# Seven products of a block pair summed in PSUM chains, pairs interleaved, and rotated q fetched in fewer transfers

## The chip, the cores and the metric

The kernel runs on one core of a Trainium2 chip. The metric is device time in microseconds for one execution; lower is better. Before the change it is 1741.86 us (median of three runs, 1740.02 to 1743.96). The core has five engines with a queue each: TensorE (PE, matrix products), VectorE (DVE), ScalarE (ACT), GpSimd (POOL) and SyncE (SP), which here issues nearly all transfers. Products land in PSUM, eight banks of 128 x 512 fp32; VectorE and ScalarE read them there.

## The reference

One gated block on x of 1024 positions by 1024 channels: a normalised x times a wide weight `w_in`, whose columns feed two branches, an mLSTM (a) and a differential attention (b), which are mixed, projected and normalised.

```python
h = rmsnorm(x, norm_g[layer])
proj = jnp.einsum('bsd,de->bse', h, w_in[layer])
(a_q, a_k, a_v, a_o, a_z, a_g, b_q, b_k, b_v, b_z, g_a, g_b) = jnp.split(proj, _split_points(), axis=-1)
qk = jax.nn.silu(centred_depthwise_conv(jnp.concatenate([a_q, a_k], axis=-1), ml_conv_w[layer]))
...
y_a = hm * jax.nn.sigmoid(a_o) * jax.nn.silu(a_z)
...
dq = apply_rope(b_q.reshape(B, S, DA_HEADS, 2, DA_QK_DIM), positions)
dk = apply_rope(b_k.reshape(B, S, DA_HEADS, 2, DA_QK_DIM), positions)
att = diff_attention(dq, dk, da_v, lam)
...
mix = (jax.nn.sigmoid(g_a + gb[0]) * jnp.einsum('bsc,cd->bsd', y_a, w_branch_a[layer])
       + jax.nn.sigmoid(g_b + gb[1]) * jnp.einsum('bsc,cd->bsd', y_b, w_branch_b[layer]))
x = x + jnp.einsum('bsd,de->bse', mix, w_out[layer])
return rmsnorm(x, final_g)
```

## The kernel before

Every fp32 product is made of three fast ones: each operand is split into a high part (`H`) and a rest (`L`), and H x H, H x L and L x H are summed in one PSUM bank. The program is one list of units for TensorE, cut into stages: an opening that normalises x and makes the first gate projections (up to about 70 us), the **pair phase** (70 to 410 us), the **attention stage** (410 to about 1145 us), then the mLSTM, the mix and the output.

**Pair phase.** The columns of a_q, a_k (which go through the convolution), a_o and a_z are worked on in 16 pairs of 128-column tiles. A pair is a 2 x 2 block product (two column tiles by two halves of the positions, with the 1024 rows of the weight in two halves), done in seven products f = 0 to 6 in place of eight, in Winograd's form. `load_form` (L223) makes the weight of a product: POOL adds or subtracts tiles of `raw` (into `s1f`, `s2f`, `s3f`), ACT rounds the result into H (L256), and VectorE (f = 0, 4, 6) or POOL subtracts to get L (L258). `pair_units` (L261) runs a product as two units of six 128x512 matmuls into a bank of its own (L279); the tag `T` has six banks. The four outputs (i, j) are sums of products: ACT copies the first product to `p1` (L285), and VectorE adds products to `u2` and `u3` (L282) and adds the last one to each output in the sink. `oz_sink` (L307) makes o and z: VectorE adds (L318), ACT takes tanh (L321, L326), VectorE combines (L319). `conv_sink` (L334) writes a half row of `cin` (L344), and when both halves are there it convolves: ACT multiplies by the first tap into an accumulator in another `T` bank (L358), VectorE adds four taps (L360), ACT takes tanh (L361), VectorE makes y (L363), ACT and POOL split it (L366, L369) and SP stores it. Convolution pairs and o/z pairs alternate. Small units for the gates and the rope angles lie between products by the table at L1536.

**Attention stage.** For each of eight heads, `da_proj` (L829) projects q and k in two column sets and two halves (`first`, `second`) into two alternating `pj` banks, rotates them (VectorE L839, L840, L852, L853; POOL L854, L855; ACT L857; POOL L858, into one buffer `hl`), writes `hl` to DRAM in four transfers (`stk`, L861) and reads it back in another layout: keys with one transfer (`kst`, L862) and queries with four (`qH`, `qL`, L865) for a half. `zz` (L869) makes the gate z: ACT tanh L871, then VectorE L872, in `zg`. The scores are matmuls at L912; VectorE takes a row maximum (`nm`, L914), ACT the exponential (L916), VectorE combines two softmaxes (L923), TensorE transposes, ACT and VectorE split (`pH` L936, `pL` L937), and TensorE multiplies by v (`PV`, L948). The norm of a head is spread over partitions by way of DRAM (`rb<-rsd`, L987), and `scale` (unit G, one for each half, L991) multiplies it into `zg` and SP stores the result (`yb`, L992). `weave` lays the projections of the next head between the steps t = 0 to 7 of a head's cycle (`da_cycle`, L1009).

From the opening's end on, only TensorE keeps the order in which the program is written (`keep(E.PE)`, L1529); for ACT, VectorE, POOL and SP a scheduler sets the order by its own estimate of times. Each engine then works strictly down its list, and SP too: a transfer that must wait holds up those behind it.

Of the kernel before, what the change touches and what calls it, by code (L numbers as in the profile page):

```python
# [109 lines left out]
class Block:  # L110
    def __init__(self, tc, A):
# [5 lines left out]
        self.ml, self.opening, self.terms = False, True, {}  # L117
# [54 lines left out]
    def load_w(self, key):  # L172
# [33 lines left out]
        self.wt[key] = (wH, wL)  # L206

# [15 lines left out]
    def load_form(self, key):  # L223
# [3 lines left out]
        if f == 0:  # L227
            self.pair_raws(p + 1)
        r1, r2 = self.praws[p]
        tag = "wH" if (7 * p + f) % 2 == 0 else "wL"  # L230
# [5 lines left out]
        if f == 0:  # L236
            src = r1[:, lo]
        elif f == 1:
            self.s1f, self.s2f = tmp("s1f"), tmp("s2f")
            g.tensor_tensor(out=self.s1f, in0=r2[:, lo], in1=r2[:, hi], op=ALU.add)  # L240
            sub(self.s2f, self.s1f, r1[:, lo])
            src = self.s2f
        elif f == 2:
            src = tmp("s3f")
            sub(src, r1[:, lo], r2[:, lo])
        elif f == 3:
            src = self.s1f
        elif f == 4:
            src = r1[:, hi]
        elif f == 5:  # L250
            src = self.s2f
            sub(src, r1[:, hi], src)
        else:
            src = r2[:, hi]
            del self.praws[p]
# [3 lines left out]
        self.wt[key] = (H, Lo)  # L259

    def pair_units(self, p, sink):  # L261

# [8 lines left out]
        def product(f, k0):  # L271
            bH, bL = plan()[f]
            if k0 == 0:
                box["ps"] = self.bank("T")
            ps = box["ps"]
            wH, wL = self.wt[("sw", p, f)]
            for k in range(k0, k0 + 2):
                for m, (l, r) in enumerate(((wH, bH), (wH, bL), (wL, bH))):
                    self.t.matmul(ps, lhsT=l[:, k, :], rhs=r[:, k, :], start=(k == 0 and m == 0), stop=(k == 3 and m == 2))  # L279
            if k0 == 0:  # L280
                return
            add = lambda out, x: v.tensor_tensor(out=out, in0=ps, in1=x, op=ALU.add)  # L282
            if f == 0:
                box["p1"] = u("p1", 2)
                a.copy(box["p1"], ps)  # L285
            elif f == 1:
                box["u2"] = u("u2")
                add(box["u2"], box["p1"])
            elif f == 2:
                box["u3"] = u("u3")  # L290
                add(box["u3"], box["u2"])
            elif f == 3:
                add(box["u2"], box["u2"])
                sink(1, 1, ps, box["u3"])
# [4 lines left out]
            elif f == 6:  # L299
                sink(1, 0, ps, box["u3"])  # L300

        return [Unit(6 * MM, lambda f=f, k0=k0: product(f, k0), (("sw", p, f),)) for f in range(7) for k0 in (0, 2)]
# [4 lines left out]
    def oz_sink(self, i0):  # L307
# [4 lines left out]
        def sink(i, j, ps, rest):  # L312
# [5 lines left out]
            v.tensor_tensor(out=ps, in0=ps, in1=rest, op=ALU.add)  # L318
# [15 lines left out]
    def conv_sink(self, seg, n):  # L334
# [3 lines left out]
        def sink(i, j, ps, rest):  # L338
# [5 lines left out]
            v.tensor_tensor(out=raw[:, 2 + j * 512:2 + (j + 1) * 512], in0=ps, in1=rest, op=ALU.add)  # L344
# [6 lines left out]
            for half in range(2):  # L351
# [4 lines left out]
                acc = self.bank("T")  # L356
# [16 lines left out]
    def run(self, units):  # L373
# [10 lines left out]
        for i, u in enumerate(units):  # L384
            if u.keys:
# [4 lines left out]
                while nxt < len(order) and (order[nxt] in self.loaded or not self.opening  # L390
                                            and (order[nxt][0] != "sw" or hasattr(self, "_s0")) and ahead(order[nxt])):
                    if order[nxt] not in self.loaded:
                        self.load_w(order[nxt])
# [435 lines left out]
    def da_proj(self, h, st):  # L829
# [12 lines left out]
        def second(half, pb):  # L842
# [3 lines left out]
            qH = w1.tile([128, 2, 512], F32R, name="qH", tag="qH", bufs=3)  # L846
            qL = w1.tile([128, 2, 512], F32R, name="qL", tag="qL", bufs=3)
            st["q", half] = (qH, qL)
# [11 lines left out]
            for g in range(4):  # L860
                q.dma_start(out=dr[g].rearrange("c i s -> i c s"), in_=fb(hl[32 * g:32 * g + 32]))  # L861
            q.dma_start(out=fb(st["k"][:, :, c]), in_=dr[2:4].rearrange("j c i s -> (c i) j s"))  # L862
# [16 lines left out]
        for half in range(2):  # L879
            z[(half + 1) * self.PIECES - 1].after = ((("G", h - 1, half), LAG["G"]),)  # L880
# [128 lines left out]
    def da_cycle(cur, prev, t):  # L1009
# [8 lines left out]
        if prev and t in (4, 5):  # L1018
            un.append(prev["G"](t - 4))
# [623 lines left out]
```

## Time and profile before

| | |
|---|---|
| median of three runs | 1741.86 us (1740.02 to 1743.96) |
| the profiled execution, its time / its span | 1743.21 us / 1741.4 us |
| mean granted TensorE clock | 0.988 |
| VectorE, busy / instructions | 1045.8 us (60%) / 1919 |
| ScalarE, busy / instructions | 768.8 us (44%) / 1524 |
| GpSimd, busy / instructions | 601.3 us (35%) / 608 |
| HBM read / written | 143.47 MB / 63.05 MB |

The span runs from the first to the last instruction; the execution's own time is 1.8 us more. Instruction rows give the start, the duration, the engine, the line, and what was read and written; a bracket behind a row gives how long the engine had been idle and what released it. Busy shares are means over stages with different limits, so each stage is read on its own.

### The profile page before, as it was taken

How to read it: one execution, taken by the hardware profiler on the slowest of the kernel's cores; microseconds unless marked ns; L12 is line 12 of the kernel's file. 1: busy time of each engine (PE TensorE's matmuls, PEld its weight loads, DVE VectorE, ACT ScalarE, POOL GpSimd, SP SyncE). 2: the span in 40 equal slices, each digit the busy share in tenths (PEclk: the TensorE clock that was granted, in tenths of full speed). 3: DMA queues.
4: the chain of work that ended last, by engine and by line, in shares of the span. 5: the costliest groups of instructions: out<-in, count | busy, mean ns of one | idle time of the engine just before them, and what ended most of it. 6: DMA issues, size and time to landing. Idle time of an engine off the chain costs nothing. (4 is left out here: it accounts for less than half of the span.)

```text
span 1741.4 us, 24821 instructions
## 1 busy us (share of the span) xinstructions
PE 1663.4 (96%) x9119; PEld 1418.1 (81%) x9119; DVE 1045.8 (60%) x1919; ACT 768.8 (44%) x1524; POOL 601.3 (35%) x608
## 2 busy tenths in 40 slices
PE   7999999999999999999999989999999988999998
PEld 6777877787887987798789878889998866888887
DVE  5788888894266666666666655424666743226533
ACT  7444445443255444454445544424655743122211
POOL 4766665664332224322441331222312311222000
PEclk9999999999999999999999999999999999999999
DMA  5343434344533514441534162156454327444222
GB/s 180 93 136 110 134 109 133 110 139 128 145 87 90 145 55 105 117 126 41 148 94 134 38 163 67 61 156 194 137 158 155 97 76 253 134 137 142 85 85 85
DMA packets 190603, 208.14 MB, mean 120 GB/s; under 512 B 12761, under 2 KB 136050, under 8 KB 190482
## 3 DMA queue, kind: packets, MB, share of 16 engines
q1 hardware_dynamic: 189570, 204.98, 39.3%
q8 instruction: 72, 1.18, 0.3%
q10 hardware_dynamic: 912, 1.59, 0.2%
q14 instruction: 49, 0.40, 0.1%
HBM read 143.47 MB, written 63.05 MB: 119 GB/s over the span
## 5 line engine op out<-in xcount | busy, mean ns | idle before, releaser
L416 PE MATMUL pj<-hH,wH 128*128 128x512 f32 x640 | 257.6, 403 | 4.6 <-ACT wH L188 3.1
L416 PE MATMUL pj<-hH,wL 128*128 128x512 f32 x640 | 252.1, 394 | 1.6 <-POOL wL L202 1.0
L416 PE MATMUL pj<-hL,wH 128*128 128x512 f32 x640 | 252.1, 394 | 0.2 <-DVE hL L567 0.2
L916 ACT ACTIVATE e<-S,nm 128x1024 f32<-128x1024 f32 x128 | 143.1, 1118 | 179.5 <-DVE nm L914 179.1
L204 POOL TENSOR_TENSOR wL<-raw,wH 128x1024 fp32r<-128x1024 f32 x41 | 99.6, 2428 | 315.6 <-ACT wH L199 312.1
L937 DVE TENSOR_TENSOR pL<-T,pH 128x512 fp32r<-128x512 f32 x128 | 87.8, 686 | 141.7 <-ACT pH L936 141.7
L914 DVE TENSOR_REDUCE nm<-S 128x1 f32<-128x1024 f32 x128 | 155.6, 1216 | 20.9 <-PE S L912 20.8
L438 PE MATMUL pj<-wH,hH 128*128 128x256 f32 x512 | 147.7, 288 | 0.2
L438 PE MATMUL pj<-wL,hH 128*128 128x256 f32 x512 | 145.0, 283 | 1.7 <-POOL wL L202 1.7
L416 PEld LDWEIGHTS pj<-hH,wL 128*128 128x128 f32 x640 | 121.0, 189 | 29.6 <-POOL wL L202 2.2
L416 PEld LDWEIGHTS pj<-hH,wH 128*128 128x128 f32 x640 | 121.4, 190 | 28.5 <-ACT wH L188 3.5
L438 PE MATMUL pj<-wH,hL 128*128 128x256 f32 x512 | 144.6, 282 | 0.0
L416 PEld LDWEIGHTS pj<-hL,wH 128*128 128x128 f32 x640 | 121.4, 190 | 23.2 <-DVE hL L567 0.6
L416 PE MATMUL pj<-sl_yb,wH 128*128 128x512 f32 x384 | 121.8, 397 | 5.1 <-ACT sl_yb L1321 2.2
L199 ACT CAST wH<-raw 128x1024 fp32r<-128x1024 f32 x56 | 58.8, 1049 | 125.1 <-PE pj L416 108.0
L438 PEld LDWEIGHTS pj<-wL,hH 128*128 128x128 f32 x512 | 97.8, 191 | 2.5 <-POOL wL L202 2.5
L438 PEld LDWEIGHTS pj<-wH,hH 128*128 128x128 f32 x512 | 98.0, 191 | 1.6 <-ACT wH L199 0.6
L438 PEld LDWEIGHTS pj<-wH,hL 128*128 128x128 f32 x512 | 97.8, 191 | 0.9
L912 PE MATMUL S<-kst,qH 128*128 128x512 f32 x256 | 90.1, 432 | 6.2 <-DMA kst<-stk 6.2
L360 DVE SCALAR_TENSOR_TENSOR T<-cin,cols,T 128x512 f32<-128x512 f32 x128 | 89.2, 749 | 7.1 <-ACT T L358 6.2
L923 DVE SCALAR_TENSOR_TENSOR e<-e,r,e 128x1024 f32<-128x1024 f32 x64 | 92.6, 1447 | 1.3
L416 PEld LDWEIGHTS pj<-sl_yb,wH 128*128 128x128 f32 x384 | 73.3, 191 | 23.2 <-DVE sl_yb L1322 3.4
(359 smaller groups left out, 4213.2 us busy)
## 6 DMA issues: line engine op xcount, KB each, us to landing
raw<-in_w_in_dram SPq DMA_DIRECT2D x88, 512.0 KB, 4.0
stk<-hl SPq DMA_DIRECT2D x64, 256.0 KB, 3.7
qH<-stk SPq DMA_DIRECT2D x32, 256.0 KB, 5.1
qL<-stk SPq DMA_DIRECT2D x32, 256.0 KB, 5.3
kst<-stk SPq DMA_DIRECT2D x16, 512.0 KB, 4.3
x<-in_x_dram SPq DMA_DIRECT2D x8, 512.0 KB, 9.3
cak<-y SPq DMA_DIRECT2D x16, 256.0 KB, 4.3
cakH<-cin SPq DMA_DIRECT2D x16, 256.0 KB, 2.0
```

The costliest lines, as they stand in the source:

```text
L199: self.a.copy(wH, raw)
L204: self.p.tensor_tensor(out=wL, in0=raw, in1=wHf, op=ALU.subtract)
L360: v.scalar_tensor_tensor(out=acc, in0=raw[:, o + x:o + x + 512], scalar=w(x), in1=acc, op0=ALU.mult, op1=ALU.add)
L416: self.t.matmul(ps, lhsT=l[:, k, :], rhs=r, start=(n == 0), stop=(n == 23))
L438: self.t.matmul(ps[:, i, :], lhsT=l, rhs=r[:, k, :], start=(kh == 0 and k == 0 and m == 0), stop=(kh == 1 and k == 3 and m == 2))
L912: self.t.matmul(ps[:, o], lhsT=x[:, j, c], rhs=st["k"][:, j, o], start=first, stop=not first)
L914: v.tensor_reduce(out=nm, in_=ps, axis=AX.X, op=ALU.max, negate=True)
L916: a.activation(out=e, in_=ps, func=AF.Exp, bias=nm[:, 0:1], accum_out=Z[:, j, t:t + 1])
L923: v.scalar_tensor_tensor(out=e0, in0=e, scalar=r[:, 0:1], in1=e0, op0=ALU.mult, op1=ALU.add)
L937: v.tensor_tensor(out=pL[:, :, s], in0=ps, in1=pH[:, :, s].bitcast(F32), op=ALU.subtract)
```

## The change

- **Chains.** Products f = 0, 1, 2, 6 now accumulate one after another in one bank (X), f = 3, 5 in a second (G), and f = 4 stands alone in a third (F); only f = 0, 3 and 4 open a bank. ACT copies X out after f = 0, 1 and 2 (`p1`, `u2`, `u3`). Output (1,1) is G after f = 3 plus `u3`; (0,0) is F plus `p1`; (0,1) is G after f = 5 plus `u2`; (1,0) is X after f = 6 as it stands, with no sum (ACT copies it to `cin` for the convolution, or takes tanh directly). The three additions of L282 are gone, and so is one of four in the sinks.
- **Overlap.** TensorE's order for pair x and the pair y before it is x0, y6, x3, y5, x1, x4, x2. After the last pair y6 and y5 follow with nothing between.
- **Banks.** The convolution's accumulators and the (1,1) sum of o and z move from `T` to the two `pj` banks.
- **Forms.** `s1f` is made for f = 3 and used again for f = 1. The raw weights of pair p + 2 are fetched after the form of f = 5 of pair p. The places of the small units move with the new order.
- **Rotated q.** `qH` and `qL` become one tile `qq`; two transfers for a half in place of four, and `kst` follows them.
- **Order in the attention stage.** For head 0 the q, k projection runs whole, then z (before: half of q, k, then z, then the other half). G of the second half is written at step t = 6 in place of 5, and its due time for z's second half is halved. The next raw weight is fetched when a weight is split (`ahead`).

```diff
     def pair_units(self, p, sink):
...
-            if k0 == 0:
-                box["ps"] = self.bank("T")
-            ps = box["ps"]
+            name, first = "XXXGFGX"[f], f in (0, 3, 4)
+            if k0 == 0 and first:
+                box[name] = self.bank("T")
+            ps = box[name]
...
-            add = lambda out, x: v.tensor_tensor(out=out, in0=ps, in1=x, op=ALU.add)
-            if f == 0:
-                box["p1"] = u("p1", 2)
-                a.copy(box["p1"], ps)
-            elif f == 1:
-                box["u2"] = u("u2")
-                add(box["u2"], box["p1"])
-            elif f == 2:
-                box["u3"] = u("u3")
-                add(box["u3"], box["u2"])
-            elif f == 3:
-                add(box["u2"], box["u2"])
-                sink(1, 1, ps, box["u3"])
+            if f < 3:
+                n = ("p1", "u2", "u3")[f]
+                box[n] = u(n, 1 + (f == 1))
+                a.copy(box[n], ps)
+                if f == 2:
+                    sink(1, 1, box["G"], box["u3"])
             elif f == 4:
                 sink(0, 0, ps, box["p1"])
             elif f == 5:
                 sink(0, 1, ps, box["u2"])
             elif f == 6:
-                sink(1, 0, ps, box["u3"])
+                sink(1, 0, ps, None)
...
-                acc = self.bank("T")
+                acc = self.psA.tile([128, 512], F32, name="pj", tag="pj", bufs=2)
...
+            for o in range(2):
+                q.dma_start(out=fb(qq[64 * o:64 * o + 64]), in_=dr[0:2].rearrange("j (p c) i s -> (c i) (j p) s", p=2))
             q.dma_start(out=fb(st["k"][:, :, c]), in_=dr[2:4].rearrange("j c i s -> (c i) j s"))
-            for o in range(2):
-                for x, y in ((qH, 0), (qL, 2)):
-                    q.dma_start(out=fb(x[64 * o:64 * o + 64]), in_=dr[0:2, y:y + 2].rearrange("j c i s -> (c i) j s"))
...
-            for i in range(len(self.pairs)):
-                for k, u in enumerate(self.pair_units(i, sinks[i])):
+            products = [self.pair_units(i, sinks[i]) for i in range(len(self.pairs))]
+            for i, x in enumerate(products + [None]):
+                y = products[i - 1] if i else None
+                un = sum(([x[0]] if x else []) + ([y[6]] if y else []) + ([x[3]] if x else []) + ([y[5]] if y else [])
+                         + ([x[1], x[4], x[2]] if x else []), [])
...
-            w.add(*qk[0][:c], *z[0], *qk[0][c:], *self.da_v(0, sts[0:2]))
+            w.add(do(lambda: setattr(self, "ahead", True)), *qk[0], *z[0], *self.da_v(0, sts[0:2]))
```

The change moves work on engines whose order the scheduler sets. At three places the lists of before and after read as follows (a row is a line, an operation, what it writes and reads, its shape, and a count where it repeats).

**ScalarE in the pair phase**, around a convolution pair that is followed by an o/z pair. Before (T is a bank, p the copy of the first product, `cin` and y the convolution's rows, raw, s1f, s2f, s3f the sources of a weight form):

```order
L285 COPY p_1582<-T 128x512
L256 CAST wH<-raw 128x512
L256 CAST wL<-raw 128x512
L256 CAST wH<-s2f 128x512
L256 CAST wL<-s3f 128x512
L256 CAST wH<-s1f 128x512
L358 ACTIVATE T<-cin,cols 128x512
L256 CAST wL<-raw 128x512
L358 ACTIVATE T<-cin,cols 128x512
L361 ACTIVATE tz<-T 128x512
L256 CAST wH<-s2f 128x512
L366 CAST cin<-y 128x512
```

After, from the copy of X to `cin` (L352) on (L366 and L369 are the first tap and the tanh; `u_1789` at L293 is the `u2` of the next pair):

```order
L352 COPY cin<-T 128x512
L257 CAST wH<-raw 128x512
L366 ACTIVATE pj<-cin,cols 128x512 x2
L257 CAST wL<-raw 128x512
L257 CAST wH<-s1f 128x512
L369 ACTIVATE tz<-pj 128x512 x2
L293 COPY u_1789<-T 128x512
L374 CAST cin<-y 128x512
L366 ACTIVATE pj<-cin,cols 128x512
```

The sums that VectorE made at L282 are copies on ScalarE now, and the `u2` copy stands behind the two tanh of the pair before, which wait for VectorE's eight taps.

**SP where a head with an odd number gives way to the next** (stk is the rotated q, k on its way to DRAM; rb the spread norm; yb a finished half of the head before). Before:

```order
L987 DMA rb<-rsd 128x512
L861 DMA stk<-hl 32x4x512
L992 DMA yb_91<-zg 128x512
L987 DMA rb<-rsd 128x512
L861 DMA stk<-hl 32x4x512
L992 DMA yb_91<-zg 128x512
L861 DMA stk<-hl 32x4x512 x2
L865 DMA qH<-stk 64x2x512
L865 DMA qL<-stk 64x2x512
L862 DMA kst<-stk 128x2x512
```

After:

```order
L993 DMA rb<-rsd 128x512
L868 DMA stk<-hl 32x4x512
L998 DMA yb_91<-zg 128x512
L993 DMA rb<-rsd 128x512
L868 DMA stk<-hl 32x4x512 x3
L870 DMA qq<-stk 64x4x512 x2
L871 DMA kst<-stk 128x2x512
L166 DMA raw<-in_w_in_dram 128x4x256
L998 DMA yb_91<-zg 128x512
```

The second store of `yb`, which waits for the second G on VectorE, stood ahead of two `stk` and of `kst`; it now stands behind them.

**VectorE at the first projections of the attention stage** (m and hl are the rotation's products, zg the gate, pj a bank). Before:

```order
L839 TENSOR_TENSOR m_3772<-pj,cosT 128x512
L840 TENSOR_TENSOR m_3773<-pj,sinT 128x512
L852 TENSOR_TENSOR hl<-pj,sinT 128x512
L853 TENSOR_TENSOR hl<-pj,cosT 128x512
L872 SCALAR_TENSOR_TENSOR zg<-zg,pj 128x512 x2
L839 TENSOR_TENSOR m_3904<-pj,cosT 128x512
L840 TENSOR_TENSOR m_3905<-pj,sinT 128x512
```

After:

```order
L859 TENSOR_TENSOR hl<-pj,sinT 128x512
L860 TENSOR_TENSOR hl<-pj,cosT 128x512
L847 TENSOR_TENSOR m_3767<-pj,cosT 128x512
L848 TENSOR_TENSOR m_3768<-pj,sinT 128x512
L878 SCALAR_TENSOR_TENSOR zg<-zg,pj 128x512
L859 TENSOR_TENSOR hl<-pj,sinT 128x512
L860 TENSOR_TENSOR hl<-pj,cosT 128x512
L878 SCALAR_TENSOR_TENSOR zg<-zg,pj 128x512
```

The first half of z is finished ahead of the rotation's second pair of products, which read the bank that z's second half is to use. From the v projection of head 0 on, TensorE's list is the same in both kernels to the end.

More of the change, by code (lines that the diff above doesn't have):

```diff
@@ L343, in sink @@
             raw, got = box[i]
[L344 removed]
+            part = raw[:, 2 + j * 512:2 + (j + 1) * 512]
+            if rest is not None:
+                v.tensor_tensor(out=part, in0=ps, in1=rest, op=ALU.add)
+            else:
+                a.copy(part, ps)
             got.append(j)
```

60 lines of the change are left out of this document (34 added, 26 removed).

## The prediction

> **What bounds the kernel.** The first part of the page, the busy time of each engine, puts TensorE far ahead:
>
> ```profile
> PE 1663.4 (96%) x9119; PEld 1418.1 (81%) x9119; DVE 1045.8 (60%) x1919; ACT 768.8 (44%) x1524; POOL 601.3 (35%) x608
> ```
>
> The change removes no matmul, so only TensorE's idle time and its slow clock can be won. The list of waits, in TensorE's part (what it waited for; total us, times, longest), says how much there is:
>
> ```profile
> PE PV L948 <- DVE pL L937: 6.6, 3, 2.4
> PE S L912 <- DMA kst<-stk: 6.2, 3, 2.7
> PE T L279 <- DVE cin L344: 6.1, 2, 4.1
> PE T L279 <- DVE y L363: 4.2, 5, 1.7
> PE T L279 <- POOL wL L258: 1.3, 1, 1.3
> ```
>
> The third and fourth rows are the pair phase waiting for a bank, 10.3 us in seven waits. The second is three heads waiting for keys. The windows table (busy us and count for PE, PEld, DVE, ACT, POOL, then granted clock, DMA share, GB/s) gives the pair phase and the two stretches of it at half clock:
>
> ```profile
> 88.00:410.00 322.00, 310.84 (x1326) 244.89 (x1325) 275.13 (x416) 152.41 (x261) 202.49 (x179) 0.98 0.39 126
> 137.90:144.73 6.83, 4.85 (x12) 3.82 (x13) 6.79 (x11) 2.54 (x5) 0.00 (x0) 0.50 0.28 78
> 308.56:311.97 3.41, 3.19 (x9) 1.98 (x8) 3.40 (x6) 1.39 (x3) 0.45 (x1) 0.50 0.56 154
> ```
>
> VectorE is busy 275 of 322 us here, 85%, and the timeline at the longest wait shows what follows from that (start, duration, engine, line, operation, idle time before it and its releaser):
>
> ```profile
> 131.39 2.79 DVE L733 TENSOR_TENSOR_SCAN gch<-gch 32x256 f32<-32x256 f32 x2
> ...
> 137.59 1.55 DVE L360 SCALAR_TENSOR_TENSOR T<-cin,cols,T 128x512 f32<-128x512 f32 x2 [0.90 <-ACT T L358]
> ...
> 139.05 0.68 DVE L344 TENSOR_TENSOR cin<-T,u 128x512 f32<-128x512 f32 x1
> ...
> 139.88 0.76 PE L279 MATMUL T<-hH,wL 128*128 128x512 f32 x1 [4.11 <-DVE cin L344]
> ```
>
> Scans for the gates and then convolution taps stand ahead of the output sum at L344, and as long as that sum has not read its bank, TensorE has no free one among the six. It is a queue on VectorE that has turned into a shortage of banks. The half clock came with it. At full clock matmuls start 0.23 us apart:
>
> ```profile
> 304.56 0.40 PE L279 MATMUL T<-TL,wH 128*128 128x512 f32 x1
> 304.79 0.40 PE L279 MATMUL T<-TH,wH 128*128 128x512 f32 x1
> ```
>
> The 12 matmuls of the first slow stretch had 4.85 us and needed 12 x 0.23 = 2.8, the 9 of the second had 3.41 and needed 2.1: 2.05 + 1.3, so **3.4 us** lost to the clock.
>
> **The pair phase.** What the edit takes from VectorE and gives to ScalarE is counted with these groups (busy us, mean ns; then idle time before them):
>
> ```profile
> L360 DVE SCALAR_TENSOR_TENSOR T<-cin,cols,T 128x512 f32<-128x512 f32 x126 | 87.7, 749 | 6.2 <-ACT T L358 5.4
> L282 DVE TENSOR_TENSOR u<-T,u 128x512 f32<-128x512 f32 x30 | 20.5, 682 | 9.1 <-PE T L279 8.6
> L282 DVE TENSOR_TENSOR u<-T,p 128x512 f32<-128x512 f32 x15 | 10.2, 682 | 0.0
> L344 DVE TENSOR_TENSOR cin<-T,u 128x512 f32<-128x512 f32 x22 | 15.0, 683 | 0.0
> L258 DVE TENSOR_TENSOR wH<-raw,wH 128x512 fp32r<-128x512 f32 x21 | 23.4, 1115 | 2.5 <-ACT wH L256 2.4
> L361 ACT ACTIVATE tz<-T 128x512 f32<-128x512 f32 x32 | 19.1, 596 | 31.3 <-DVE T L360 30.0 <-DVE wL L258 0.6 <-DMA cakL<-tz 0.4
> L285 ACT COPY p<-T 128x512 f32<-128x512 f32 x15 | 8.7, 581 | 1.0 <-PE T L279 1.0
> ```
>
> In this window 45 additions of L282 go (30.7 us), and 15 sink sums at about 0.68 (10.3 us): VectorE falls from 275 to about 234 us. ScalarE gains two copies a pair and one for half the pairs, some 38 x 0.581 = 22 us, and stands near 175. Both have room. A pair now opens three banks in place of seven, and the convolution's accumulators use the idle `pj` banks, so a sum may be late by a whole pair before TensorE lacks one of the six. I take the **10.3 us of bank waits and the 3.4 us of slow clock as gone**, and half of the 1.3 us wait for POOL in the first pair, because its f = 3 needs one POOL operation less now: 0.6. Together 14.3.
>
> What comes in their place is waits on the chain, since X can't be added to while ScalarE copies it. A product is 12 x 0.23 = 2.8 us. In the steady order x1, x4, x2 the `u2` copy has the whole of x4 to hide behind. Its worst place is behind a convolution pair, where the ScalarE list has two tanh ahead of it. Counted from the end of y6: the copy to `cin` and the first taps end near 2.2, the eight VectorE taps take 8 x 0.749 = 6.0 us and end near 7.7, the second tanh near 8.4, the `u2` copy near 9.2; x1 ends at 3 x 2.8 = 8.4 and x2 starts at 11.2. That leaves 2.0 us. In the same way the `u3` copy has x0 of the next pair to hide behind (2 us left) and the (1,1) sum that must read G has x0, y6 and x3 (some 3 us). So nothing in the steady state. For gates and angles that get in between on VectorE, the rows nearest are the scans above (2.8 us) and the copies at L642:
>
> ```profile
> L642 DVE COPY rep<-an 128x512 f32<-128x512 f32 x4 | 5.0, 1250 | 0.0
> ```
>
> Two of these in a row are 2.5 us against 2.0 of room, so 0.5 each time; I put **2 us** on all of them, between 0 and 6. At the end of the phase the cover is gone: x2, y6 and y5 follow directly. y6 waits for the `u3` copy (0.58 and a signal, 0.8 us), x2 for a late `u2` copy behind convolution work on ScalarE (about 1.0), y5 for VectorE to end the last convolution and read G (two sums of 0.68 and a wait, 1.5): **3.3 us**, between 2 and 6. For a slow clock behind that I add 0.5, between 0 and 3.4 (the loss before). The weights' other dates I cost at nothing: a tile of `raw` lands 4.0 us after its issue, and is now asked for behind the last form of the pair two before, some four products (11 us) ahead of its own first form; without that cover each pair would wait up to 4 us.
>
> ```profile
> raw<-in_w_in_dram SPq DMA_DIRECT2D x88, 512.0 KB, 4.0
> ```
>
> The phase: 14.3 - 2 - 3.3 - 0.5 = **8.5 us less**.
>
> Whether such a wait slows the clock is not certain, and here a rule bears on it. A wait of 1.69 us was followed by full clock, one of 2.00 us, like the one of 4.11, by half:
>
> ```profile
> 264.41 0.50 PE L279 MATMUL T<-hH,wL 128*128 128x512 f32 x1 [1.69 <-DVE y L363]
> ...
> 262.00:270.00 8.00, 6.31 (x28) 4.79 (x27) 7.92 (x14) 5.17 (x9) 5.13 (x4) 1.00 0.54 180
> ...
> 307.19 0.47 PE L279 MATMUL T<-hH,wL 128*128 128x512 f32 x1 [2.00 <-DVE cin L344]
> ```
>
> The Trainium skill, "TensorE: Matmul & The Clock Gate", section "HAM oscillation", asks for an idle gap over about 3.4 us before the clock drops, so by it no new wait costs clock and the sum would be 1 us lower. The trace disagrees: half clock began 1.4 us behind the wait of 2.00 us at 307.19. I keep the trace's allowance.
>
> **The attention stage.** SP works in order, and at three head boundaries it was held by the second `yb`:
>
> ```profile
> 687.23 0.65 SPq L987 DMA_DIRECT2D rb<-rsd  x1
> ...
> 692.54 0.75 DVE L991 SCALAR_TENSOR_TENSOR zg<-zg,cols,rb 128x512 f32<-128x512 f32 x1 [2.67 <-DMA rb<-rsd]
> 693.32 0.32 SPq L992 DMA_DIRECT2D yb<-zg  x1
> 693.68 0.94 SPq L861 DMA_DIRECT2D stk<-hl  x2
> 698.26 0.39 SPq L862 DMA_DIRECT2D kst<-stk  x1
> 705.27 0.50 PE L912 MATMUL S<-kst,qH 128*128 128x512 f32 x1 [2.11 <-DMA kst<-stk]
> ```
>
> The last two `stk` left at 693.68 because `yb` waited for L991. In the new order they follow `rb` (issued at 687.23) and would be out by about 690, so `kst` is issued some 4 us earlier, over the 2.1 us that TensorE waited (longest of the three: 2.7). The merged q transfers put as many bytes ahead of `kst` in fewer issues, at nothing. **All three waits go: 6.2 us** (0 if something else is then late by as much). L991 itself stands where it stood on VectorE, ahead of `pL`, and the spread `rb` leaves no earlier. So this wait and its two sisters (6.6 us in the list above) stay:
>
> ```profile
> 695.74 0.58 PE L948 MATMUL PV<-pL,vH 128*128 128x256 f32 x1 [2.18 <-DVE pL L937]
> ```
>
> New is a wait at head 0. With q, k whole ahead of z, the bank of z's second half is the one that the rotation's second half still reads, and VectorE's list finishes z's first half ahead of it. These rows price the steps:
>
> ```profile
> 433.19 0.59 ACT L871 ACTIVATE zg<-pj 128x512 f32<-128x512 f32 x1
> ...
> 433.82 0.69 DVE L872 SCALAR_TENSOR_TENSOR zg<-zg,pj 128x512 f32<-128x512 f32 x1 [5.47 <-ACT zg L871]
> ...
> 443.35 0.69 DVE L852 TENSOR_TENSOR hl<-pj,sinT 128x512 f32<-128x512 f32 x1 [4.08 <-PE pj L416]
> 443.95 0.68 DVE L853 TENSOR_TENSOR hl<-pj,cosT 128x512 f32<-128x512 f32 x1
> ```
>
> From the end of z's first half: tanh 0.59, L872 0.69, the two products to the end of the second 1.28, and signals 0.3: **2.9 us**, plus 0.5 for the clock (2 to 5 in all). The attention stage: 6.2 - 2.9 - 0.5 = **2.8 us less**. Behind it TensorE's list is the same to the end; the rest I take at nothing.
>
> **Sum.** The profiled execution took 1743.2 us (span 1741.4 and 1.8 around it): 1743.2 - 8.5 - 2.8 = 1731.9. It lies 1.35 above the median of 1741.86, so against the median the forecast is **1730.5 us**.
>
> **Rivals.**
> - *The head boundaries gain too* (with G a step later in the program and transfers moved, VectorE no longer waits for `rb`): the 6.6 us of `pL` waits go and about 2 us of slow clock behind the first of them (6.83 us at half clock as in the pair phase, where that cost 2.05), 1730.5 - 8.6 = 1722. Against it stands VectorE's unchanged order there. 0.12.
>
> ```profile
> 694.27:701.10 6.83, 5.37 (x20) 4.98 (x21) 3.45 (x6) 2.16 (x4) 1.94 (x1) 0.50 0.96 250
> ```
>
> - *The gain only moves.* The `pj` banks are two, now shared by accumulators and the (1,1) sums; if the sum waits for an accumulator, G is read late and y5 waits. Its room is 3 us; 1.3 us over it in each of eight convolution pairs is 10 us, and the time is 1740.5. 0.13.
> - *ScalarE becomes the bound, slower than before.* The `u2` copy stands behind two tanh that wait for VectorE's taps; ScalarE idled 30.0 us for exactly this before. If weight forms (1.1 us) or scans get between the eight taps, so that they end 4.5 us later than walked, x2 waits 2.5 us in eight pairs, 20 us, and half of these waits cost 1.3 of clock, 5: 1755.5. It turns to a loss from 3.4 us late on (1.4 us in eight pairs eats the 11.3). Against it: VectorE drops to three quarters busy. 0.09.
> - *The keys are not what is late* at the boundaries: 6.2 us less gain, 1736.7. 0.04.
>
> **How the numbers follow.** The forecast case has 0.62 and its own range is 1725 to 1737 (end and angles 5 us better or worse, clock 1 or 2). The low end takes in the first rival, 1721; the high end the moved gain, 1742. A measurement tells a change from 0.2%, 3.5 us, on. Faster: 0.62 + 0.12 + 0.04 = 0.78; same 0.13; slower 0.09.
>
> **What would show it.** In the profile after, no wait of L286 (the products) on `cin` or y; full clock from 90 to 380 us; VectorE near 234 us in that stage; waits of X on the copies only at its end; no S wait on `kst`; a wait near 3 us at the first z. Many short waits on the `u2` copy behind convolution pairs would prove me wrong by the third rival, and a wait of S on something other than keys by the last.

## The result, and the profile after

| | before | after |
|---|---|---|
| median of six runs | 1741.15 us (1740.02 to 1743.96) | 1731.01 us (1729.77 to 1736.47) |
| ratio | | 0.9948 (0.993 to 0.9965) |
| span of the profiled execution | 1741.4 us | 1730.0 us |
| VectorE / ScalarE busy | 1045.8 / 768.8 us | 998.4 / 783.6 us |

The change makes the kernel faster by 10.1 us, 0.5%. The forecast was 1730.5.

TensorE's list is the same from the v projection of head 0 to the end, and all profiles hold 9119 matmul records, so the start of the same matmul, counted from the end, can be compared across kernels. That divides the span into the stretches below, worked out from the records' starts. A holds the opening and the pair phase and ends in the middle of head 0's projections, where the count is the same and the order is not; B holds z of head 0; C the wait near 470 us; "to D" what lies between that and D; D the three head boundaries and what lies between them; E the mLSTM up to the mix; F the rest. The last three numbers are the boundaries alone, a part of D.

```
us                  A     B     C     to D   D      E     F      (of D: the three boundaries)
before            423.2  33.4  24.3  196.4  452.3  349.5  262.3   30.6  15.6  15.0
after             416.4  35.1  24.5  197.1  448.1  346.9  261.8   27.9  15.1  13.8
after minus before -6.8  +1.7  +0.2   +0.7   -4.2   -2.6   -0.5
```

The waits of TensorE up to 420 us in the profile after (what it waited for; total us, times, longest) answer to the bank waits of before:

```profile
PE T L131 <- DVE gc_negM L810: 4.7, 1, 4.7
PE T L286 <- ACT u L293: 2.0, 3, 1.1
PE T L286 <- POOL wL L259: 0.8, 1, 0.8
PE T L286 <- DVE pj L321: 0.6, 1, 0.6
PE T L286 <- DVE cin L350: 0.6, 2, 0.4
```

The 10.3 us of waits on `cin` and y are down to 0.6. The first row is new and is one single wait. The windows table shows the stage and the half clock behind that wait (busy us and count for PE, PEld, DVE, ACT, POOL, clock, DMA share, GB/s):

```profile
88.00:400.00 312.00, 304.71 (x1311) 242.81 (x1309) 230.51 (x354) 165.80 (x296) 201.58 (x178) 0.99 0.40 125
268.72:275.55 6.83, 5.00 (x13) 3.47 (x14) 3.76 (x13) 3.24 (x6) 4.49 (x5) 0.50 0.60 204
```

VectorE is busy 230.5 of 312 us, 74%. The timeline around the new wait:

```profile
264.71 0.21 DVE L810 COPY gc_negM<-T 128x32 f32<-128x32 f32 x1
264.83 4.05 DVE L368 SCALAR_TENSOR_TENSOR pj<-cin,cols,pj 128x512 f32<-128x512 f32 x6
...
270.20 0.21 DVE L810 COPY gc_negM<-T 128x32 f32<-128x32 f32 x1
270.30 0.30 DVE L810 COPY gc_sint<-T 128x32 f32<-128x32 f32 x2
```
```profile
259.91 0.33 PE L131 MATMUL T<-ident,gch 64*128 64x64 f32 x2
...
261.77 0.33 PE L131 MATMUL T<-ident,gch 64*128 64x64 f32 x2
...
263.62 0.33 PE L131 MATMUL T<-ident,gch 64*128 64x64 f32 x2
...
270.55 0.44 PE L131 MATMUL T<-ident,gch 64*128 64x64 f32 x2 [4.70 <-DVE gc_negM L810]
```

Small units transpose the gate columns (`gch`) into T banks, and VectorE copies them out (L810). The second copy of the first unit takes 0.21 us but stands behind six convolution taps, so its bank comes free 5.5 us after the first copy. Meanwhile three units hold a bank each that has not been read, and the fourth, which asks at 265.85 (270.55 less its wait), finds none: the pair's own three (X, G and F, which opened at 264.19) make up the six by the order of the products.

At the head boundary SP reads as the new order had it, but one wait for keys is left. SP's rows and TensorE's, after:

```profile
682.10 0.31 SPq L868 DMA_DIRECT2D stk<-hl  x1
682.46 0.43 SPq L998 DMA_DIRECT2D yb<-zg  x1
682.94 0.71 SPq L993 DMA_DIRECT2D rb<-rsd  x1
683.68 2.14 SPq L868 DMA_DIRECT2D stk<-hl  x3
687.98 1.24 SPq L870 DMA_DIRECT2D qq<-stk  x2
689.56 0.39 SPq L871 DMA_DIRECT2D kst<-stk  x1
...
690.56 0.50 SPq L998 DMA_DIRECT2D yb<-zg  x1
```
```profile
690.48 0.39 PE L954 MATMUL PV<-pL,vH 128*128 128x256 f32 x1 [2.39 <-DVE pL L943]
...
698.37 0.97 PE L918 MATMUL S<-kst,qq 128*128 128x512 f32 x3 [1.31 <-DMA kst<-stk]
```

From the first `stk` to the `kst` issue it takes 7.5 us, before 11.9 (686.34 to 698.26). Yet the score product waits again.

### The profile page after: what moved, and what is told of

It is laid out like the page before. It is cut to its first block, busy times and chain, and to the rows that moved or that the text cites. A ratio compares the mean times of both kernels' runs of the same rounds, so it can differ in the third digit from the quotient of the medians.

```text
span 1730.0 us, 24692 instructions
## 1 busy us (share of the span) xinstructions
PE 1661.3 (96%) x9119; PEld 1417.5 (82%) x9119; DVE 998.4 (58%) x1855; ACT 783.6 (45%) x1562; POOL 603.4 (35%) x608
## 5 line engine op out<-in xcount | busy, mean ns | idle before, releaser
L424 PE MATMUL pj<-hH,wH 128*128 128x512 f32 x640 | 257.7, 403 | 6.3 <-ACT wH L188 3.1
L424 PE MATMUL pj<-hH,wL 128*128 128x512 f32 x640 | 252.6, 395 | 2.6 <-POOL wL L202 1.7
L424 PE MATMUL pj<-hL,wH 128*128 128x512 f32 x640 | 252.4, 394 | 0.2 <-DVE hL L575 0.2
L918 PE MATMUL S<-kst,qq 128*128 128x512 f32 x512 | 151.4, 418 | 1.3 <-DMA kst<-stk 1.3
L424 PEld LDWEIGHTS pj<-hH,wH 128*128 128x128 f32 x640 | 121.6, 190 | 31.1 <-ACT wH L188 3.5
L424 PEld LDWEIGHTS pj<-hH,wL 128*128 128x128 f32 x640 | 121.2, 189 | 30.8 <-POOL wL L202 3.1
L424 PEld LDWEIGHTS pj<-hL,wH 128*128 128x128 f32 x640 | 121.3, 189 | 23.4 <-DVE hL L575 0.6
L424 PE MATMUL pj<-sl_yb,wH 128*128 128x512 f32 x384 | 120.7, 394 | 4.4 <-ACT sl_yb L1327 2.3
L918 PEld LDWEIGHTS S<-kst,qq 128*128 128x128 f32 x512 | 90.6, 193 | 15.3 <-DMA kst<-stk 1.8
L189 POOL TENSOR_TENSOR wL<-raw,wH 128x512 fp32r<-128x512 f32 x32 | 40.7, 1290 | 154.5 <-ACT wH L188 149.1
```

The lines of the kernel that those rows point to most:

```text
L189: self.p.tensor_tensor(out=vw(wL), in0=src, in1=vw(wHf), op=ALU.subtract)
L424: self.t.matmul(ps, lhsT=l[:, k, :], rhs=r, start=(n == 0), stop=(n == 23))
L918: self.t.matmul(ps[:, o], lhsT=x[:, j, c], rhs=st["k"][:, j, o], start=first, stop=not first)
```

## The experiments

Each kernel is compared by its time and by the stretches, because the clock moves E by several us whatever the kernel (below).

```
us                      A     B     C     D     E     half clock in E  (of D: boundaries)   median
a1 changed, again     416.7  35.1  24.6  447.2  344.6    6.8          27.5  14.9  13.5  1735.21
a2 columns later      412.5  35.1  24.6  446.9  350.6   16.8          27.1  15.0  13.6  1731.25
a3 z between          417.1  33.4  20.6  447.8  349.9   17.1          27.2  15.0  13.3  1729.43
a4 both               412.5  33.4  22.2  447.5  344.9    6.8          27.1  15.6  13.6  1720.82
b1 keys first         416.0  35.1  18.6  441.8  349.8   17.1          22.1  11.3  13.1  1721.27
b2 no overlap         427.7  35.1  25.0  446.5  349.2   13.7          26.2  15.3  12.6  1744.17
b3 pair phase only    416.6  33.4  23.8  452.2  352.1   13.7          29.6  16.6  14.4  1738.00
b4 attention only     422.6  33.4  20.6  447.6  350.7   13.7          27.4  15.4  13.6  1736.99
c1 keys, columns, z   411.6  33.4  18.6  443.3  345.7    6.8          22.1  11.3  13.1  1714.42
c2 columns spread     410.5  33.4  18.6  441.8  348.9   13.7          22.1  11.3  13.1  1713.43
c3 four reads         417.0  35.1  24.6  446.4  349.5   13.7          26.4  15.2  12.6  1733.46
c4 second G early     416.2  35.1  24.6  459.2  349.7   17.1          32.0  19.1  15.1  1745.38
```

**a1: the changed kernel again.**

> The changed kernel once more, beside the others. Theory: the gain of 11 us in the profiles of before and after is 4.2 us up to head 1 and about 3 us at the three head boundaries, and the 3.5 us that came up behind 1200 us, where TensorE's list is the same, are where the slow clock happened to fall. Then this profile has its half-clock stretches at other places, and the time from the first mLSTM product to the end differs by 1 to 4 us between the two profiles of this same kernel. Rival: those 3.5 us belong to the change; then that part of the span is the same in both profiles to within 0.5 us. Time 1731.

Measured 1735.21 us (1728.95 to 1737.3, six runs), ratio 0.9955 (0.994 to 0.9969). E is 344.6 us where the first profile of the same kernel had 346.9, and before had 349.5: the theory holds. Over the profiles E goes with the time at half clock in it: 344.6 to 345.7 us with 6.8 us of it, 346.9 with 10.2, 348.9 to 350.7 with 13.5 to 17.1; b3 alone has more, 352.1. Kernels that hold the whole change, some with an edit more, stand on both sides of before's 349.5. So the 2.6 us that E seemed to win is no gain of the change. At the first boundary a1 kept full clock, where the first profile went to half behind the wait for pL, and paid in waiting for the keys instead:

```profile
690.64 0.39 PE L954 MATMUL PV<-pL,vH 128*128 128x256 f32 x1 [2.11 <-DVE pL L943]
...
698.35 0.98 PE L918 MATMUL S<-kst,qq 128*128 128x512 f32 x3 [2.72 <-DMA kst<-stk]
```

The keys land at the same time in both; how long TensorE waits for them depends on how slowly it came there. The wait is not the price, the date of the keys is.

**a2: the gate columns one pair later.**

```diff
-((9, 8), 1, columns)
+((10, 8), 1, columns)
```

> The small units that turn the gate columns (four pairs of 64-column transposes, each with a T bank and a VectorE copy) stand one pair later, (10, 8) in place of (9, 8), where VectorE has o/z sums and no convolution taps ahead of the copies. Theory: chains keep five of six T banks taken, so a unit that needs a bank waits for VectorE's copy behind six taps: the 4.70 us wait near 270 us goes, and with it the 6.83 us of half clock (2.6 us): 7 us less than a1, 1724. Rival: the chains leave no bank free anywhere, and the wait comes back at the new place: the same time as a1 within 2 us.

Measured 1731.25 us (1727.37 to 1732.22), ratio 0.9932 (0.9921 to 0.9944), against 1735.21 for a1. A is 4.2 us shorter, not 7. The unit that had waited was the fourth, and the chains held three of the six banks there, not five. The wait of 4.7 us and the 6.83 us of half clock there are gone, but two shorter waits stand at the new place, with another, shorter half clock behind:

```profile
284.56 0.34 PE L131 MATMUL T<-ident,gch 64*128 64x64 f32 x2 [1.04 <-DVE oz L323]
...
285.47 0.47 PE L286 MATMUL T<-hH,wL 128*128 128x512 f32 x1 [0.57 <-DVE gc_negM L810]
```

Banks are short there too, but VectorE has only o/z work. The theory holds with a smaller number; and E had 10 us more at half clock than a1, which hid the gain in the spans of the two profiles (1727.2 and 1729.4).

**a3: z between the halves of head 0's q and k**, as before.

```diff
-            w.add(do(lambda: setattr(self, "ahead", True)), *qk[0], *z[0], *self.da_v(0, sts[0:2]))
+            c = len(qk[0]) // 2
+            w.add(do(lambda: setattr(self, "ahead", True)), *qk[0][:c], *z[0], *qk[0][c:], *self.da_v(0, sts[0:2]))
```

> Head 0's projections in the order of before (half of q and k, z, the other half), all else as changed. Theory: the 1.4 us wait of z's second half near 432 us goes: 1 to 2 us less than a1, 1729.5. Rival: q and k whole ahead of z bring head 0's keys earlier and this is worth more than the wait: 1 to 4 us more than a1.

Measured 1729.43 us (1726.98 to 1730.89), ratio 0.9923 (0.991 to 0.9936). B falls to the 33.4 of before: the wait cost 1.7. Not expected was C, 4.0 us shorter: in this kernel's ScalarE list the rounding of head 1's rotation weights (L188) stands ahead of the first exponential, and the 3.1 us wait for it is gone. That is the scheduler's doing and no part of either theory.

**a4: a2 and a3 together.**

> Both edits of a2 and a3. Theory: the two waits are 150 us apart and the gains add up: 8 to 9 us less than a1, 1722.5. Rival: the wait that is removed first lets TensorE run into another that was hidden behind it: less than 6 us in all.

Measured 1720.82 us (1718.61 to 1723.05), ratio 0.9877 (0.9865 to 0.989). A and B are those of a2 and a3, so the parts add up: 4.2 + 1.7, and 2.4 in C. The median is 14.4 below a1's, more than the parts, since a1's own median was 4 us above its first one; the spans of the two profiles are 7.9 apart.

**b1: the keys first.**

```diff
-            for g in range(4):
+            for g in (2, 3, 0, 1):
                 q.dma_start(out=dr[g].rearrange("c i s -> i c s"), in_=fb(hl[32 * g:32 * g + 32]))
+            q.dma_start(out=fb(st["k"][:, :, c]), in_=dr[2:4].rearrange("j c i s -> (c i) j s"))
             for o in range(2):
                 q.dma_start(out=fb(qq[64 * o:64 * o + 64]), in_=dr[0:2].rearrange("j (p c) i s -> (c i) (j p) s", p=2))
-            q.dma_start(out=fb(st["k"][:, :, c]), in_=dr[2:4].rearrange("j c i s -> (c i) j s"))
```

> The changed kernel with the key rows of the rotated tile written first and the key read (kst) ahead of the two q reads. Theory: in the changed kernel all 1 MB of q stands ahead of kst in the queue, where before it was half of it, so kst still lands 13.1 to 16 us after the first stk and the score product waits (5.1 us in three waits in the run a1). With the keys first kst is issued and lands some 3 us earlier: no wait of S on kst, and 3 to 5 us less at the three head boundaries together than in a1, where they take 27.5, 14.9 and 13.5 us. Rival: what makes the boundary late is the earlier wait for pL (6.2 us in a1), and kst is only the last of several: S then waits for q or for the softmax, and the three boundaries stay within 1 us of a1.

Measured 1721.27 us (1719.93 to 1724.84), ratio 0.9861 (0.9841 to 0.9882). No wait for keys is left, and D is 5.4 us shorter than a1's; the boundaries alone are 9.4 shorter (46.5 and 55.9), about twice what the theory said. SP at the first boundary:

```profile
667.88 0.34 SPq L998 DMA_DIRECT2D yb<-zg  x1
668.27 0.43 SPq L993 DMA_DIRECT2D rb<-rsd  x1
675.02 2.88 SPq L868 DMA_DIRECT2D stk<-hl  x4
679.19 0.38 SPq L869 DMA_DIRECT2D kst<-stk  x1
...
681.49 1.25 SPq L871 DMA_DIRECT2D qq<-stk  x2
```

`kst` goes out 4.2 us after the first `stk`, not 7.5. But this run doesn't test the keys alone: the scheduler also put the second `rb` ahead of all four `stk`, so VectorE no longer waits for it, and the waits for pL (6.2 us in a1) went too. They came back in part as two waits for the gate's bank ("PE pj L424 <- DVE zg L878: 5.6, 3, 2.1", one of the three being that of B). And C is 6.0 us shorter, by the same move on ScalarE's list as in a3. So theory and rival may both have had a hand in it, and this run can't say how much each.

**b2: chains without overlap.**

```diff
-                un = sum(([x[0]] if x else []) + ([y[6]] if y else []) + ([x[3]] if x else []) + ([y[5]] if y else [])
-                         + ([x[1], x[4], x[2]] if x else []), [])
+                un = sum(([y[6], y[5]] if y else []) + ([x[0], x[3], x[1], x[4], x[2]] if x else []), [])
```

> The chains with pairs one after the other: order 0, 3, 1, 4, 2, 6, 5 of each pair, everything else as changed. Theory: what hides the copies is the work of the neighbour pair; without it every pair pays what the end of the pair phase pays in the changed kernel (0.68 us for the u3 copy and 0.63 us for the read of G), 16 x 1.3 = 21 us, and the slow clock comes on top: 20 to 30 us more than a1, 1750 to 1760. Rival, by my forecast for the end of the phase: 3.3 us in every pair, 50 us more, 1780. Second rival: the copies are short enough not to matter and the overlap is worth under 5 us.

One execution, 1744.17 us. A is 11.0 us longer than a1's. The wait on the copy and one of its fifteen places:

```profile
PE T L286 <- ACT u L293: 11.1, 15, 1.6
```
```profile
303.56 0.59 ACT L293 COPY u<-T 128x512 f32<-128x512 f32 x1 [1.80 <-PE T L286]
...
304.20 0.50 PE L286 MATMUL T<-TH,wL 128*128 128x512 f32 x1 [0.68 <-ACT u L293]
```

Every pair pays the bare copy, 0.68 us, between f = 2 and f = 6. The read of G costs nothing here: while TensorE does f = 6, VectorE has time for the sum. So the theory and the first rival were too high and the second rival too low: the overlap is worth 11 us, and without it the pair phase is 4.5 us longer than before the change (A 427.7 and 423.2).

**b3: the pair phase alone**, with the attention stage of before (the edits to `da_proj`, `da_cycle`, `ahead` and the list of head 0 undone).

> The changed pair phase (chains, overlap, banks, forms, places of the small units) with the attention stage of before. Theory: its own gain up to the first q, k projection is about 6.8 us in the profiles of before and after, made of some 14 us won and a new wait of 4.7 us with 2.6 us of slow clock near 270 us: 5 to 9 us less than before, 1735.5. Rival: most of the gain is the attention stage's: under 4 us.

Measured 1738.0 us (1733.09 to 1742.48, ten runs), ratio 0.9965 (0.9948 to 0.9981). A is 416.6, 6.6 us below before, while the median is only 4.4 below. By the stretch the theory holds. E had 2.6 us more than before in this profile, and here the clock is not why: the time at half clock is the same (13.7 and 13.5 us), and TensorE's waits for VectorE on `W`, a tile of the mLSTM, are longer (7.4 us, before 5.1). Its key waits were 6.7 us.

**b4: the attention stage alone**, on the pair phase of before, with z between the halves.

> The attention stage's edits (one q tile, two q reads, keys behind them, second G a step later, the next raw weight fetched early; z between the halves of q and k as before) on the pair phase of before. Theory: the three head boundaries gain 3 to 5 us together, as between the profiles of before and after, and nothing else moves: 3 to 5 us less than before, 1738. Rival, by my forecast: all 6.2 us of kst waits go: 6 to 7 us less. Second rival: these edits win nothing by themselves: within 1.5 us of before.

Measured 1736.99 us (1734.43 to 1740.93), ratio 0.9954 (0.9934 to 0.9975). D is 4.7 us shorter than before, C 3.7 as in a3. Key waits fell from 6.2 to 2.5 us and did not vanish, and the waits for pL grew from 6.6 to 8.0: the theory holds for D, my forecast's 6.2 does not. That nothing else would move was wrong, since C did.

**c1: keys first, columns later, z between.**

> The edits of a2, a3 and b1 together. Theory: the gains are at three places and add up in TensorE's path: 4.2 us at the columns (pair phase 416 to 412), 1.7 us at z, some 2 to 4 us in the wait near 465 us, 8 to 10 us at the head boundaries: 1731 - 17 = 1714 give or take the slow clock's 3. Rival: b1's gain came with its own order of ScalarE in the stage before head 0 (its wait near 465 us was gone, worth 6 us), and together with a3 there is nothing left to win there: 1718 to 1721, no better than a4 or b1.

Measured 1714.42 us (1711.38 to 1718.0), ratio 0.9841 (0.9823 to 0.9858). A, B, C and D are those of a2, a3 and b1 within 1.5 us: the gains add up, with C won once.

**c2: as c1, the columns spread.**

```diff
-((10, 8), 1, columns)
+((9, 8), 3, columns)
```

> As c1, but the column units keep their start (9, 8) and stand three places apart in place of one. Theory: what makes the 4.7 us wait is that the third unit asks for a T bank while the copies of the two before it stand behind six taps on VectorE; 4 us apart each bank is read before the next is asked for, so in the midst of the taps there is still no wait over 1 us, and the pair phase ends like c1's or 1 us earlier. Rival: it is the taps as such, and any column unit in a convolution stretch waits up to 4 us: the pair phase ends 3 to 5 us later than c1's.

Measured 1713.43 us (1710.12 to 1715.33), ratio 0.9832 (0.9817 to 0.9848); A 410.5. The units stand in the midst of the taps, the first two at 260.05 and 264.70, and none of their transposes waits. The third and the fourth, and VectorE:

```profile
269.35 0.33 PE L131 MATMUL T<-ident,gch 64*128 64x64 f32 x2
...
273.97 0.33 PE L131 MATMUL T<-ident,gch 64*128 64x64 f32 x2
```
```profile
264.97 4.05 DVE L368 SCALAR_TENSOR_TENSOR pj<-cin,cols,pj 128x512 f32<-128x512 f32 x6
268.93 0.21 DVE L810 COPY gc_negM<-T 128x32 f32<-128x32 f32 x1
...
272.36 0.30 DVE L810 COPY gc_sint<-T 128x32 f32<-128x32 f32 x2
```

The same copy stands behind the same six taps as in the changed kernel (4.05 us), and it costs nothing: the third unit comes at 269.35, just behind it, and when the fourth comes at 273.97 the banks of the first two have been read. In the changed kernel the fourth unit asked at 265.85, while that copy was still 4.4 us away and none of the three banks before it had been read. It was the number of banks held at once, not the taps. c2 is the fastest version of the study, 28 us below before; c1 and c2 can't be told apart by their medians.

**c3: q in four reads, keys behind them.**

```diff
-                q.dma_start(out=fb(qq[64 * o:64 * o + 64]), in_=dr[0:2].rearrange("j (p c) i s -> (c i) (j p) s", p=2))
+                for x in range(2):
+                    q.dma_start(out=fb(qq[64 * o:64 * o + 64, x::2]), in_=dr[0:2, 2 * x:2 * x + 2].rearrange("j c i s -> (c i) j s"))
```

> The changed kernel with q read in four transfers into the one tile, keys still behind them. Theory: the merging is worth nothing, since kst waits for the bytes ahead of it and not for the number of reads: the head boundaries (27.5, 14.9, 13.5 us in a1) within 1 us in all. Rival: two issues fewer ahead of kst (about 0.6 us each) bring it 1.2 us forward at each boundary: 2 to 4 us more than a1 in all.

One execution, 1733.46 us, with D at 446.4, 0.8 below a1. The three boundaries are 54.2 us, 1.7 below a1 and so outside the theory's 1 us, but b2, with q in two reads, has 54.1. The number of reads is worth nothing that shows; "fewer transfers" is not where the gain came from.

**c4: the second G early.**

```diff
-        if prev and t in (4, 6):
-            un.append(prev["G"](t // 2 - 2))
+        if prev and t in (4, 5):
+            un.append(prev["G"](t - 4))
```

with the old due time for z and the end at six steps again.

> The changed kernel with G of the second half at step 5 and its old due time, so that SP has the second yb ahead of two stk again. Theory: the place of yb is what the boundaries gained by: S waits for kst again as before or longer (all of q is now ahead of it), the three boundaries take 61 us or more together as before (30.6, 15.6 and 15.0) against 55.8 in a1. Rival: the place of yb doesn't matter: within 1 us of a1.

One execution, 1745.38 us, 10 us above a1's median; D is 12.0 us longer than a1's. The three boundaries take 66.2 us, 10.3 more than in a1. Of these, by the records' durations, 4.7 are idle time of TensorE and 5.7 its clock: 13.5 us of the boundaries are at half clock, in a1 none. TensorE's wait for keys, and SP's rows:

```profile
PE S L918 <- DMA kst<-stk: 9.8, 3, 5.1
```
```profile
687.47 0.32 SPq L998 DMA_DIRECT2D yb<-zg  x1
687.83 1.27 SPq L868 DMA_DIRECT2D stk<-hl  x2
689.21 2.08 SPq L870 DMA_DIRECT2D qq<-stk  x2
692.46 0.39 SPq L871 DMA_DIRECT2D kst<-stk  x1
```

With the second `yb` ahead of two `stk` again the boundaries lose more than the change had won: with all of q ahead of the keys, the waits are 9.8 us where the kernel before had 6.2. Without the new place of `yb` there is no gain at the boundaries, and the longer key waits point to q ahead of the keys as what takes a part of it back.

## Why the prediction was right, point by point

The time, the direction and the size came out, and most of the mechanisms, but the closeness is luck. Up to the end of D the change won 8.4 us of the 11.3 forecast; the other 3.1 of the 11.5 between the two spans fell in E and F, where nothing was changed, and the same kernel's median was 1735.21 in a1. Within the sum, the small units were some 5 us worse than forecast and the keys 1 to 2, and the end of the phase and z were each some 2 us better. Two of the signs that the prediction named did not show: half clock came at 268.72, and S still waited for `kst`.

- **Bank waits and slow clock in the pair phase: right.** 10.3 us of waits on `cin` and y became 0.6, and neither stretch of half clock is left. VectorE came to 230.5 us against a forecast of 234. A as a whole fell by 6.8 us where 8.5 were forecast; the next two points are the rest of the sum.
- **The small units: mis-sized, and for a wrong reason.** I allowed 2 us for gates and angles, after "a sum may be late by a whole pair before TensorE lacks one of the six". That step failed. It counts the banks of pairs alone. A pair opens three banks and not seven, but it holds them long, all three at once from f = 4 on, and the small units take a bank each: three of them in a row, unread, and the fourth finds none. It measured 4.7 us of wait and 2.6 us of clock: the lead over before, taken at the same count of matmuls from the end, falls from 8.2 us ahead of the place to 0.9 behind it. a2 and c2 show that the place of the units decides it (4.2 and 6.2 us of A against a1).
- **The end of the phase: too dear.** Forecast 3.3 us, measured 0.68 for the copy and 0.63 for the read of G. b2 confirms that the bare copy is 0.68 wherever nothing lies between.

```profile
397.17 0.50 PE L286 MATMUL T<-TH,wH 128*128 128x512 f32 x1 [0.68 <-ACT u L293]
...
400.85 0.50 PE L286 MATMUL T<-hH,wL 128*128 128x512 f32 x1 [0.63 <-DVE pj L321]
```

- **The steady state: right but for two places.** The `u2` copy behind two tanh, the mechanism of the slower rival, was late once, by 0.20 us (at 146.55). The longer wait, 1.10 us, came another way:

```profile
152.31 0.62 ACT L257 CAST wH<-s2f 128x512 fp32r<-128x512 f32 x1 [3.02 <-POOL s2f L238]
152.83 0.58 ACT L293 COPY u<-T 128x512 f32<-128x512 f32 x1
...
153.47 0.50 PE L286 MATMUL T<-TH,wL 128*128 128x512 f32 x1 [1.10 <-ACT u L293]
```

  Here it was a weight's rounding, late from POOL, that stood ahead of the copy on ScalarE, and not a tanh.
- **z of head 0: half the size.** Forecast 2.9 and 0.5 for the clock, measured 1.41 of wait and 1.7 in B. I had the second half of z wait for the rotation's bank; it waited for its own first half's (tanh and L878, 0.60 + 0.69), and the rotation's products ran beside it.

```profile
431.13 0.60 ACT L877 ACTIVATE zg<-pj 128x512 f32<-128x512 f32 x1 [4.61 <-PE pj L424]
431.76 0.69 DVE L878 SCALAR_TENSOR_TENSOR zg<-zg,pj 128x512 f32<-128x512 f32 x1 [10.15 <-ACT zg L877]
432.36 0.68 DVE L859 TENSOR_TENSOR hl<-pj,sinT 128x512 f32<-128x512 f32 x1
432.50 0.50 PE L424 MATMUL pj<-hH,wH 128*128 128x512 f32 x1 [1.41 <-DVE zg L878]
```

- **The keys: the earlier issue right, its worth too large.** Forecast 6.2 us, D gave 4.2 (a1: 5.1), with 1.3 to 5.1 us of key waits left. What failed is "the merged q transfers put as many bytes ahead of `kst`": before, two reads of 256 KB stood ahead of it, now two of 512 KB, and in the stretch where the keys are fetched the queues are full (DMA share 0.96 in a1):

```profile
689.68:693.09 3.41, 2.45 (x18) 2.37 (x19) 2.14 (x4) 1.34 (x3) 1.44 (x1) 1.00 0.96 223
```

  The key's issue came 4.4 us sooner after the first `stk`, as forecast, and from there to the score product it took 8.3 us in place of 7.0 (690.06 to 698.35 in a1, 698.26 to 705.27 before). The list of DMA issues, with the median us from issue to landing, points the same way: b4 has all of q ahead of the keys, b1 the keys ahead of q. The traces tell only two landings in each of these runs, at places that differ, so this is no proof.

```profile
kst<-stk SPq DMA_DIRECT2D x16, 512.0 KB, 7.2
```
```profile
kst<-stk SPq DMA_DIRECT2D x16, 512.0 KB, 4.3
```

  How much of the gain is waits and how much clock differs between two profiles of the same kernel. Against before, the three boundaries have 6.1 us less idle time and 1.6 us more by the slower clock in the first profile, and 2.6 less idle time and 2.7 less by the clock in a1. Only the sum, 4.4 and 5.3 us, can be put down to the change.
- **The waits for pL stay: right** (6.6 before, 6.5 after).
- **Nothing behind the attention stage: right**, though a single pair of profiles seems to say 2.6 us. In kernels that hold the whole change E took 344.6 to 350.6 us, with before's 349.5 among them.

What stays open: in b1 the key's date and the earlier `rb` moved together, and no run separates them. Of a1's waits at the boundaries 5.0 us are for keys and 4.1 for pL, and b1 has neither.

## What to carry to other kernels

A chain in PSUM frees the engine that did the sums, but it holds its bank from the first product to the last: count banks by how long they are held, not by how many are opened, with those of small units among them, and place such units far enough apart that each is read before the next asks. A chain that is read on the way pays each read in full (0.68 us here) unless another chain's products lie between. Where several transfers feed one wait, try the order in which they are needed: it was a part of b1's gain, though not shown alone. Joining them was worth nothing with the same bytes ahead (c3).

## What the runs showed of the hardware that I had not expected

Half clock comes in stretches of 3.41 us or twice that (but for the last one of a run), and their starts lie on one grid through a whole run: in the profile after, 268.72 and 466.70 lie 58.0 times 3.413 us apart, 268.72 and 1391.71 329.0 times. Counting TensorE's busy share in each cell of that grid, over all fourteen profiles of this study, from 20 us on and without the last stretch at half clock of each run:

```
busy share of a cell at full clock    next cell at half   next cell at full
under 0.43                                   63                    0
0.43 to 0.56                                 17                   43
0.56 to 0.65                                  3                   42
over 0.65                                     0                 6676
busy share of a cell at half clock    next cell at half   next cell at full
under 0.83                                   22                    0
0.83 to 0.88                                  2                    2
over 0.88                                     0                   81
```

So a wait of 2 us costs clock or not by where it falls: the 2.39 us at the first boundary after lay, all but 0.5 us, in one cell (busy 1.50 of 3.41 us, then half clock), the 2.11 us in a1 were cut in two by a cell's edge (busy 2.26 and 2.45, full clock). These are rows of the windows table for the cell of after and the first of the two cells of a1 (the second is quoted above):

```profile
688.57:691.98 3.41, 1.50 (x12) 1.50 (x13) 2.99 (x4) 0.39 (x1) 2.25 (x1) 1.00 0.80 179
```
```profile
686.26:689.68 3.42, 2.26 (x11) 1.62 (x9) 2.24 (x3) 1.08 (x2) 0.81 (x1) 1.00 0.87 283
```

The Trainium skill, "TensorE: Matmul & The Clock Gate", section "Part 1: The HAM clock gate", has a free-running window of 3413 ns, which agrees with the grid. Its condition for the drop, at least one idle window, does not: here a busy share under 0.43 was always enough and one of 0.43 to 0.56 in 17 of 60 cells, and the way back took 0.83 or more. By these shares shorter waits that fall into one cell add up, and the same matmuls of E took 344.6 us in one profile of the changed kernel and 346.9 in the other.
